# Where the unit triangular inverse and the Newton steps of the reciprocal root keep their data

## The chip, the cores and the metric

The kernel runs on one core of a Trainium2 chip. A core has five engines that run their own instruction streams in order and meet at semaphores: TensorE (PE) multiplies matrices into PSUM, VectorE (DVE) and ScalarE (ACT) do elementwise work and reach both the large memory SBUF and the small accumulator memory PSUM, GpSimd (POOL) does elementwise work in SBUF alone, and SyncE (SP) issues most DMAs. DMAs move data between DRAM and SBUF. The metric is the device time of one execution in microseconds.

## The reference

One inference step of a two-layer recurrent trunk, for 1024 prompt rows and 8 samples of 8 rows (1088 rows of width 1024). Layer 0 has an S5 state space group and a gated delta net (GDN) side by side; layer 1 is RWKV-7 time mixing. Each is followed by a gated feed-forward block (FFN) of width 2816. Two things in it matter here.

First, GDN solves, for every chunk and head, with a unit lower triangular matrix; RWKV, done in chunks of 64 rows, needs the same:

```python
tmat = lax.linalg.triangular_solve(eye + lmat, jnp.broadcast_to(eye, lmat.shape),
                                   left_side=True, lower=True)
```

Second, every norm multiplies by a reciprocal root, `lax.rsqrt(mean(x * x) + eps)`: the RMS norms of the layers, the norms of q, k and of GDN's output, and the group norm over each 64 columns after RWKV's recurrence.

## The kernel before, in words

The rows are worked on in two halves (columns 0 to 511 and 512 to 1087 of transposed activations). Dense products take float32 weights as a high and a low part and run three matmuls for each pair (`mm`, line 322). To make the parts, ScalarE rounds a weight tile `raw` to `wh` (line 305), and GpSimd subtracts, `wl = raw - wh` (line 309), until a low part has been stored in DRAM and can be loaded in later passes.

The recurrences run in units: 8 units for GDN (4 heads, 2 halves) and 32 for RWKV (8 pairs of heads, 4 segments of time, each half of the rows having two segments). The instructions of the units and of dense work are written one after the other, and a scheduler with a simulated timeline then interleaves them when the kernel is built: on each engine, rows of a unit stand between rows of the FFN or of projections. The order is fixed before the kernel runs. The 16 RWKV units of the first half run beside layer 0's second FFN half, the 16 of the second half beside layer 1's first FFN half.

Each unit calls `Kern.inverse` (line 155). It takes the 16x16 diagonal blocks `D` out of the matrix, sends them through DRAM (`dA`) so that one block lies in one partition (`L`, 32 to 40 partitions of 256 numbers), and inverts all blocks at once by substitution: `T` starts as 16x16 identities (line 181), and 15 steps of two VectorE instructions each follow, a product into a scratch tile `Tm` (line 186) and an update of `T` in place (line 188), 15 to 64 numbers a partition. That makes 30 dependent instructions for an inverse, 1200 in all. `T` goes back through DRAM (`dT`, line 190) into `Tc`, and TensorE, VectorE and ScalarE combine blocks to 32, 64 and 128 (`py`, `tt`, `TT`). `L`, `T` and `Tm` are all in SBUF. The `py` tiles of PSUM have a tag (`gi`, `gp`, `qi`) with one buffer.

`Kern.rsqrt` (line 325) finds reciprocal roots on VectorE: an estimate from the bits of the number (two integer instructions, lines 336 and 337), then three Newton steps of three instructions each (lines 340 to 342), with the estimate `y` and a scratch `q` (whose tile is also called `g`). It is called 20 times for the layers' norms (tiles `nrm...`, 64 to 72 numbers a partition, from the PSUM tile `ss`), 32 times after RWKV's units (tiles `rgn...`, 4 to 6 numbers, out of `vr`), and 18 times elsewhere (`gq`, `go`, `kn`). All its tiles but the input `ss` lie in SBUF.

Some lines serve for comparison: 519 (`al = s*0.5 - ah`, VectorE, both tensors in SBUF), 534 (`x = x + pd`, one tensor in SBUF, one in PSUM), 1657, 1692 and 1034 (VectorE reading PSUM), 1655 (ScalarE copying from PSUM).

Of the kernel before, what the change touches and what calls it, by code (L numbers as in the profile page):

```python
# [8 lines left out]
F32 = mybir.dt.float32  # L9
F32R = mybir.dt.float32r  # L10
I32 = mybir.dt.int32
AF = mybir.ActivationFunctionType
OP = mybir.AluOpType
AX = mybir.AxisListType
PSUM = bass.MemoryType.PSUM
DRAM = bass.MemoryType.DRAM

T = 1088
NP = 1024
CW = 272  # L20
NCH = [(c, CW) for c in range(0, T, CW)]

# [82 lines left out]
class Kern:  # L105
# [49 lines left out]
    def inverse(self, gp, ps, dr, A, wd, nu, ns, sgn, tag, pb=2, own=False, TT=None):  # L155
# [4 lines left out]
        nc, v = self.nc, self.nc.vector  # L160
        nl = 8 * nu + ns
        op = OP.subtract if sgn > 0 else OP.add
        dA = dr.tile([nu + 1, 8, 256], F32, name="dA", tag="dA%d" % wd)
        size = {"mk": 320, "L": 256, "T": 256, "tt32": 160, "Y32": 160}
        kin = {"Y32": "L", "tt32": "T"}
        two = [lambda n, i=i: gp.tile([128, size[kin.get(n, n)] if own else 320], F32, name=n,
                                      tag="i" + kin.get(n, n) if own else "inv%d" % i, bufs=1) for i in range(2)]
# [9 lines left out]
            nc.sync.dma_start(dA[nu, 0:ns].rearrange("b (j i) -> (b j) i", i=16), D[0:16 * ns, nu])  # L177
        L = two[0]("L")[:8 * nu + 8, :256].rearrange("p (a b) -> p a b", b=16)
        nc.sync.dma_start(L[:nl], dA.rearrange("u b (j i) -> (u b) j i", i=16)[:nl])
        T = two[1]("T")[:8 * nu + 8, :256].rearrange("p (a b) -> p a b", b=16)  # L180
        v.tensor_copy(T[:nl], self.i16[:nl])
        m = gp.tile([8 * nu + 8, 64], F32, name="Tm", tag="invm", bufs=1)
        for j in range(15):
            n = 15 - j
            mm = m[:nl, :(j + 1) * n].rearrange("p (c i) -> p c i", i=n)
            v.tensor_mul(mm, L[:nl, j:j + 1, j + 1:16].to_broadcast([nl, j + 1, n]),  # L186
                         T[:nl, 0:j + 1, j:j + 1].to_broadcast([nl, j + 1, n]))
            v.tensor_tensor(T[:nl, 0:j + 1, j + 1:16], T[:nl, 0:j + 1, j + 1:16], mm, op=op)  # L188
        dT = dr.tile([nu + 1, 8, 256], F32, name="dT", tag="dT%d" % wd)
        nc.sync.dma_start(dT.rearrange("u b x -> (u b) x")[:nl], T[:nl].rearrange("p c i -> p (c i)"))  # L190
        Tc = gp.tile([128, nu + 1, 16], F32, name="Tc", tag="invTc", bufs=1 + own)
        nc.sync.dma_start(Tc[:, 0:nu], dT[0:nu].rearrange("u b (c i) -> (b c) u i", i=16))
        TS = None
# [19 lines left out]
        py = ps.tile([128, 2, nu, 16], F32, tag=tag, name="py", bufs=pb)  # L213
# [4 lines left out]
        for u in range(nu):  # L218
            for b in range(4):
# [3 lines left out]
                               op1=OP.add)  # L223
# [16 lines left out]
        py = ps.tile([128, nu, 32], F32, tag=tag, name="py2", bufs=pb)  # L240
# [7 lines left out]
        py = ps.tile([128, 2 if wd == 128 else 1, nu, 32], F32, tag=tag, name="py3", bufs=pb)  # L248
# [15 lines left out]
        py = ps.tile([128, 2, nu, 64], F32, tag=tag, name="py4", bufs=pb)  # L264
# [57 lines left out]
                self.nc.tensor.matmul(ps, a[k], b[:, c:c + cn], start=i == 0, stop=i == last)  # L322
                i += 1

    def rsqrt(self, pool, out, x, scale, eps, tag):

        nc = self.nc
        sh = list(x.shape)
        if scale is None:
            v = x  # L330
        else:
            v = pool.tile(sh, F32, tag=tag + "v", name=tag + "v", bufs=1)
            nc.vector.tensor_scalar(v, x, scale, eps, op0=OP.mult, op1=OP.add)
        y = pool.tile(sh, F32, tag=tag + "y", name=tag + "y", bufs=1)
        g = pool.tile(sh, I32, tag=tag + "q", name=tag + "g", bufs=1)
        nc.vector.tensor_scalar(g, v.bitcast(I32), 1, None, op0=OP.logical_shift_right)
        nc.vector.tensor_scalar(y.bitcast(I32), g, -1, 0x5F3759DF, op0=OP.mult, op1=OP.add)
        q = g.bitcast(F32)
        for i in range(3):
            nc.vector.tensor_mul(q, y, y)  # L340
            nc.vector.scalar_tensor_tensor(q, q, -0.5, v, op0=OP.mult, op1=OP.mult)
            self.last = nc.vector.scalar_tensor_tensor(out if i == 2 else y, q, 1.5, y, op0=OP.add, op1=OP.mult)

    def stats(self, xs):
# [19 lines left out]
    def norm(self, ss, qn):  # L364
        p = self.dx
        r = p.tile([128, self.width // 4], F32, tag="rst", name="rst", bufs=2)[:, :qn]
        self.rsqrt(p, r, ss[:, :qn], 1.0, 1e-6, "nrm")
        return r

    def spread(self, r):  # L370
# [835 lines left out]
class RWKV:  # L1206
# [53 lines left out]
    def open(self, ctx):  # L1260
# [20 lines left out]
        nc.vector.memset(self.halo[:, 0], 0.0)  # L1281

    def projections(self, s, x, shift0, w1, a1, g1, lw2, wk, wr, wv, unit,
                    norms, wk0):

# [152 lines left out]
        for j, wt, dst, more in ((0, wr, self.drr, {1: (0,), 2: (1,), 3: (2, 3), 4: (4, 5), 5: (6, 7)}), (3, wv, self.dv, {})):  # L1438
            hs = [mix(j, i) for i in range(2)]
            if j == 3:  # L1440
                banks = banks[:2]
            for m in range(6):
                w = K.weight(wt[m])
                for i in range(2):
                    one(dst, m, w, hs[i], i)
                for ft in more.get(m, ()):
                    second(ft)
                if j == 3:
                    unit(m)
                if j == 0 and m == 0:  # L1450
                    lora(*loras[5])
                    second = self.second(s, lw2)
                if j == 0 and m == 0:
                    for i, (c, cn) in enumerate(chunks):
                        pt = self.bank("qp")[:16, :cn]
                        for y, (b, n) in enumerate(blocks[i]):
                            nc.tensor.transpose(pt[:, b:b + n], ko[:n, 3 * i + y], K.ident[:n, :n])
                        t = K.tmp("kt")[:16, :cn]
                        nc.scalar.copy(t, pt)
                        nc.sync.dma_start(dks[:, c:c + cn], t)  # L1460
            ws = [K.weight(wt[m]) for m in (6, 7)]
            for i in range(2):
                for m in (6, 7):
                    one(dst, m, ws[m - 6], hs[i], i)
        for m in (6, 7):
            unit(m)
# [79 lines left out]
    def unit(self, ft, si, s, S0):  # L1546
        K, nc, gp, HR = self.K, self.K.nc, self.gp, self.HR
        v = nc.vector
# [8 lines left out]
        def new(name, tag="up"):  # L1557
            return gp.tile([128, 320], F32, tag=tag, name=name, bufs=RING[tag])[:, :W]
# [5 lines left out]
        k, r, vv, rkb = (new(n, "ui") for n in ("k", "r", "v", "rkb"))  # L1564
# [58 lines left out]
        pb = ptile("pb")[:, :W]  # L1623
# [19 lines left out]
        for c0, n, mk in groups:  # L1643
            g = slice(c0, c0 + n)
# [25 lines left out]
        pa, pu, pb = pc[:, 0:2], pc[:, 2], pc[:, 3:5]  # L1670
        py = self.ps.tile([128, 4, 2, 64], F32, tag="qy", name="py", bufs=1)
# [6 lines left out]
        two = lambda t: t.rearrange("p a t -> p (a t)")  # L1678
# [27 lines left out]
        parts = [(slice(0, 128), slice(0, 2))] + ([(HR[0], slice(2, 3))] if smp else [])  # L1706
        yc, sq = (gp.tile([128, 3, 2, 64], F32, tag="uy", name=n, bufs=3) for n in ("yc", "sq"))
        su, vr, rs = (gp.tile([128, 3, 2], F32, tag="u_" + n, name=n, bufs=1) for n in ("su", "vr", "rs"))
        wide = lambda t, p: t[p][:, :, :, None].to_broadcast([p[0].stop, p[1].stop - p[1].start, 2, 64])
        if smp:  # L1710
            v.memset(vr, 1.0)
        for p in parts:
            v.tensor_reduce(su[p], py[p], op=OP.add, axis=AX.X)
            v.scalar_tensor_tensor(yc[p], wide(su, p), -1.0 / 64, py[p], op0=OP.mult, op1=OP.add)
            nc.scalar.activation(sq[p], yc[p], AF.Square)
            v.tensor_reduce(vr[p], sq[p], op=OP.add, axis=AX.X)
            v.tensor_scalar(vr[p], vr[p], 1.0 / 64, 64e-5, op0=OP.mult, op1=OP.add)
        nb = W // 128 + W % 128 // 64
        K.rsqrt(gp, rs[:, :nb], vr[:, :nb], None, None, "rgn")
        pT = ptile("pT", "qp", 1)[:, :W]  # L1720
        for p in parts:
            nc.gpsimd.tensor_mul(yc[p], yc[p], wide(rs, p))
# [3 lines left out]
        g = new("g", "ul")  # L1726
# [48 lines left out]
def layer0(K, I, right, dr):  # L1775
# [19 lines left out]
    with ExitStack() as c1:  # L1795
# [27 lines left out]
        with tc.tile_pool(name="x0", bufs=4, side="right") as x0, tc.tile_pool(name="psn", bufs=2, space=PSUM) as psn:  # L1823
# [15 lines left out]
            for j, (c, cn) in enumerate(NCH):  # L1839
                if j == 0:  # L1840
                    norm(c, cn)
                    wba = K.weight(I["wba"], 8, 8, tag="wba", bufs=1)
                    ws = [K.weight(I["win"][i], bufs=2) for i in range(2)]
                if j + 1 < len(NCH):
                    norm(*NCH[j + 1])
                if j == 1:
                    s5.consts(hi[7][:, c:c + 1].bitcast(F32), *(I[k] for k in ("lre", "lim", "ls", "bre", "bim", "cre", "cim", "dsk", "h0")))
                proj(wba, lambda c, cn, ps: nc.scalar.copy(rows[:, c:c + cn], ps), 8, [(c, cn)])
                for m, w in enumerate(ws):
                    inputs(m, w, [(c, cn)])  # L1850
# [266 lines left out]
```

## Time and profile before

| | |
|---|---|
| median of 3 runs | 3689.62 us (3682.62 to 3697.84) |
| the profiled execution | 3691.23 us, its span 3689.5 us |
| mean granted TensorE clock | 0.943 |
| busy: PE, DVE, ACT, POOL | 92%, 65%, 38%, 28% of the span |

Busy PE time is the union of pipelined matmuls, so 92% is not TensorE at its peak. Three stretches of the span hold all inverses: 340 to 828 us (GDN, 8 inverses), 1374 to 2116 us (RWKV, first half, 16) and 2363 to 3140 us (RWKV, second half, 16).

### The profile page before, as it was taken

To read this page: it belongs to the slowest core of one execution; us is meant where nothing else is said; L and a number is where in the kernel's file an instruction comes from. 1 tells how busy PE (TensorE), PEld (TensorE's weight loads), DVE (VectorE), ACT (ScalarE), POOL (GpSimd) and SP (SyncE) were. 2 spreads that over 40 slices of the span, in tenths; PEclk is the share of its full clock that TensorE was granted. 3 is DMA by queue.
4 is the path that set the end of the run, shared out by engine and by line. 5 is a ranking of instruction groups with operands and counts; after the bars stand their busy time and mean duration, and the time that the engine had idled before them with its cause. 6 is when DMAs were issued, how large, how long until landed. Compare 5 with 4: busy or idle time off the path is not lost.

```text
span 3689.5 us, 77380 instructions
## 1 busy us (share of the span) xinstructions
PE 3379.0 (92%) x29894; PEld 3171.2 (86%) x29894; DVE 2394.0 (65%) x6834; ACT 1390.8 (38%) x3264; POOL 1041.0 (28%) x1037
## 2 busy tenths in 40 slices
PE   7889999999997889999999898898988989899998
PEld 6879888989997888899889888888887877799997
DVE  7886888754448556776666673577778888344344
ACT  3333333323224454444443454443443444222222
POOL 3222133223216450111010142334333332122221
PEclk8989987999998899999999999989999999899998
DMA  3434453445554585344443456722322324322322
GB/s 102 95 87 120 96 177 104 130 132 188 186 174 132 176 292 161 111 143 150 153 130 114 135 167 221 238 86 87 87 82 84 102 79 135 105 69 75 92 81 66
DMA packets 387552, 474.36 MB, mean 129 GB/s; under 512 B 142312, under 2 KB 305896, under 8 KB 387184
## 3 DMA queue, kind: packets, MB, share of 16 engines
q1 hardware_dynamic: 364144, 447.13, 39.8%
q10 hardware_dynamic: 23040, 22.29, 1.8%
q8 instruction: 235, 3.85, 0.4%
q14 instruction: 133, 1.09, 0.1%
HBM read 344.32 MB, written 123.79 MB: 127 GB/s over the span
## 4 chain that ended last, share of the span: by engine, by line
PE 54%; DVE 26%; DMA 12%; issue 3%; ACT 3%; SPq 1%; POOL 1%; DVEq 0%; ACTq 0%; POOLq 0%
PE pg L322 20%; PE pd L322 10%; PE pj L322 5%; PE po L322 4%; PE pi L322 3%; DVE T L188 3%; DVE Tm L186 3%; DVE mx L1350 1%; DMA raw<-in_wd 1%; DMA dT<-T 1%; DMA L<-dA 1%; DMA rkb<-dks 1%; DMA Tc<-dT 1%; DVE x L534 1%; DVE Z L800 1%
## 5 line engine op out<-in xcount | busy, mean ns | idle before, releaser
L322 PE MATMUL pg<-hi,wh 128*128 128x288 f32 (+1 forms) x2816 | 833.8, 296 | 23.8 <-DVE s L511 15.5
L322 PE MATMUL pg<-lo,wh 128*128 128x288 f32 (+1 forms) x2816 | 830.9, 295 | 4.4 <-DVE lo L409 3.5
L322 PE MATMUL pg<-hi,wl 128*128 128x288 f32 (+1 forms) x2816 | 827.8, 294 | 1.2 <-POOL wl L309 1.2
L309 POOL TENSOR_TENSOR wl<-raw,wh 128x1024 fp32r<-128x1024 f32 (+3 forms) x205 | 483.1, 2358 | 903.5 <-ACT wh L305 791.5
L322 PEld LDWEIGHTS pg<-hi,wh 128*128 128x128 f32 x2816 | 540.7, 192 | 32.9 <-DVE s L511 19.1
L322 PEld LDWEIGHTS pg<-lo,wh 128*128 128x128 f32 x2816 | 540.8, 192 | 12.4 <-DVE lo L409 5.2
L322 PEld LDWEIGHTS pg<-hi,wl 128*128 128x128 f32 x2816 | 540.2, 192 | 3.3 <-POOL wl L309 1.4
L305 ACT CAST wh<-raw 128x1024 fp32r<-128x1024 f32 (+3 forms) x309 | 313.2, 1014 | 362.7 <-PE pg L322 99.6
L322 PE MATMUL pd<-ah,wdh 128*128 128x256 f32 (+1 forms) x1280 | 387.2, 303 | 20.3 <-DVE x L534 16.5
L322 PE MATMUL pd<-ah,wdl 128*128 128x256 f32 (+1 forms) x1280 | 373.5, 292 | 5.9 <-DMA wdl<-low_wd 5.9
L322 PE MATMUL pd<-al,wdh 128*128 128x256 f32 (+1 forms) x1280 | 371.9, 291 | 0.0
L322 PEld LDWEIGHTS pd<-ah,wdh 128*128 128x128 f32 x1280 | 243.8, 190 | 32.0 <-DVE x L534 18.2
L322 PE MATMUL pj<-hi,wh 128*128 128x256 f32 (+1 forms) x768 | 235.5, 310 | 18.1 <-ACT hi L408 7.7
L322 PEld LDWEIGHTS pd<-ah,wdl 128*128 128x128 f32 x1280 | 243.8, 190 | 9.1 <-DMA wdl<-low_wd 7.6
L322 PEld LDWEIGHTS pd<-al,wdh 128*128 128x128 f32 x1280 | 244.2, 191 | 0.4
L322 PE MATMUL pj<-hi,wl 128*128 128x256 f32 (+1 forms) x768 | 232.2, 307 | 12.7 <-DMA wl<-low_wr 7.5
L322 PE MATMUL pj<-lo,wh 128*128 128x256 f32 (+1 forms) x768 | 235.2, 308 | 8.7 <-DVE lo L409 6.8
L534 DVE TENSOR_TENSOR x<-x,pd 128x256 f32<-128x256 f32 (+1 forms) x384 | 162.4, 426 | 92.0 <-PE pd L322 88.5
L305 ACT CAST wdh<-raw 128x384 fp32r<-128x384 f32 (+1 forms) x224 | 111.2, 497 | 258.6 <-PE pd L322 161.2
L322 PE MATMUL pi<-hi,wh 128*128 128x272 f32 x640 | 191.5, 299 | 5.0 <-ACT us L1818 3.5
L186 DVE TENSOR_TENSOR Tm<-L,T 32x15 f32<-32x15 f32 (+8 forms) x600 | 161.1, 268 | 47.6 <-DMA L<-dA 34.6
L322 PE MATMUL pi<-lo,wh 128*128 128x272 f32 x640 | 190.2, 297 | 0.0
(643 smaller groups left out, 8008.2 us busy)
## 6 DMA issues: line engine op xcount, KB each, us to landing
raw<-in_wg SPq DMA_DIRECT2D x88, 512.0 KB
raw<-in_wup SPq DMA_DIRECT2D x88, 512.0 KB
raw<-in_wd SPq DMA_DIRECT2D x192, 192.0 KB
low_wg<-wl SPq DMA_DIRECT2D x22, 512.0 KB
low_wup<-wl SPq DMA_DIRECT2D x22, 512.0 KB
wl<-low_wg SPq DMA_DIRECT2D x22, 512.0 KB
wl<-low_wup SPq DMA_DIRECT2D x22, 512.0 KB
raw<-in_win SPq DMA_DIRECT2D x20, 512.0 KB
```

The source lines that it names most:

```text
L186: v.tensor_mul(mm, L[:nl, j:j + 1, j + 1:16].to_broadcast([nl, j + 1, n]), T[:nl, 0:j + 1, j:j + 1].to_broadcast([nl, j + 1, n]))
L188: v.tensor_tensor(T[:nl, 0:j + 1, j + 1:16], T[:nl, 0:j + 1, j + 1:16], mm, op=op)
L305: nc.scalar.copy(wh, raw)
L309: (lo or nc.gpsimd).tensor_sub(wl, raw, wh)
L322: self.nc.tensor.matmul(ps, a[k], b[:, c:c + cn], start=i == 0, stop=i == last)
L534: v.tensor_add(x[m][:, c:c + cn], x[m][:, c:c + cn], ps)
L800: v.tensor_add(o, o, m1)
L1350: v.scalar_tensor_tensor(t, xx[k][:, c:c + cn], self.vec[:, j, k:k + 1], x[k][:, c:c + cn], op0=OP.mult, op1=OP.add)
```

## The change

`T` of the substitution moves to PSUM, into the tag that the `py` tiles of the same inverse use. Its start, a copy of the identities, moves from VectorE to ScalarE; after the 15 steps ScalarE copies `T` to an SBUF tile `Ts`, and the DMA to `dT` reads that. `rsqrt` takes an optional `y`, and the Newton step is written so that each instruction has `y` and at most one other tensor as inputs (`q = v*y`, `q = q*-0.5*y`, `y = (q+1.5)*y`) instead of `q = y*y`, `q = q*-0.5*v`; the first shift now writes into the bits of `y`. The layers' norms give as `y` a free part of the PSUM tile `ss`, RWKV's group norm a free part of its PSUM tile `py`, which also takes the sums `vp`. The other calls keep `y` in SBUF. The number of VectorE instructions in a root stays 11.

```diff
--- before.py
+++ after.py
@@ -177,8 +177,8 @@
             nc.sync.dma_start(dA[nu, 0:ns].rearrange("b (j i) -> (b j) i", i=16), D[0:16 * ns, nu])
         L = two[0]("L")[:8 * nu + 8, :256].rearrange("p (a b) -> p a b", b=16)
         nc.sync.dma_start(L[:nl], dA.rearrange("u b (j i) -> (u b) j i", i=16)[:nl])
-        T = two[1]("T")[:8 * nu + 8, :256].rearrange("p (a b) -> p a b", b=16)
-        v.tensor_copy(T[:nl], self.i16[:nl])
+        T = ps.tile([128, 512], F32, tag=tag, name="T", bufs=pb)[:8 * nu + 8, :256].rearrange("p (a b) -> p a b", b=16)
+        nc.scalar.copy(T[:nl], self.i16[:nl])
         m = gp.tile([8 * nu + 8, 64], F32, name="Tm", tag="invm", bufs=1)
         for j in range(15):
             n = 15 - j
@@ -187,7 +187,9 @@
                          T[:nl, 0:j + 1, j:j + 1].to_broadcast([nl, j + 1, n]))
             v.tensor_tensor(T[:nl, 0:j + 1, j + 1:16], T[:nl, 0:j + 1, j + 1:16], mm, op=op)
         dT = dr.tile([nu + 1, 8, 256], F32, name="dT", tag="dT%d" % wd)
-        nc.sync.dma_start(dT.rearrange("u b x -> (u b) x")[:nl], T[:nl].rearrange("p c i -> p (c i)"))
+        Ts = two[1]("T")[:8 * nu + 8, :256]
+        nc.scalar.copy(Ts[:nl], T[:nl].rearrange("p c i -> p (c i)"))
+        nc.sync.dma_start(dT.rearrange("u b x -> (u b) x")[:nl], Ts[:nl])
         Tc = gp.tile([128, nu + 1, 16], F32, name="Tc", tag="invTc", bufs=1 + own)
         nc.sync.dma_start(Tc[:, 0:nu], dT[0:nu].rearrange("u b (c i) -> (b c) u i", i=16))
         TS = None
@@ -322,7 +324,8 @@
                 self.nc.tensor.matmul(ps, a[k], b[:, c:c + cn], start=i == 0, stop=i == last)
                 i += 1
 
-    def rsqrt(self, pool, out, x, scale, eps, tag):
+    def rsqrt(self, pool, out, x, scale, eps, tag, y=None):
+
 
         nc = self.nc
         sh = list(x.shape)
@@ -331,14 +334,15 @@
         else:
             v = pool.tile(sh, F32, tag=tag + "v", name=tag + "v", bufs=1)
             nc.vector.tensor_scalar(v, x, scale, eps, op0=OP.mult, op1=OP.add)
-        y = pool.tile(sh, F32, tag=tag + "y", name=tag + "y", bufs=1)
-        g = pool.tile(sh, I32, tag=tag + "q", name=tag + "g", bufs=1)
+        if y is None:
+            y = pool.tile(sh, F32, tag=tag + "y", name=tag + "y", bufs=1)
+        q = pool.tile(sh, F32, tag=tag + "q", name=tag + "q", bufs=1)
+        g = y.bitcast(I32)
         nc.vector.tensor_scalar(g, v.bitcast(I32), 1, None, op0=OP.logical_shift_right)
-        nc.vector.tensor_scalar(y.bitcast(I32), g, -1, 0x5F3759DF, op0=OP.mult, op1=OP.add)
-        q = g.bitcast(F32)
+        nc.vector.tensor_scalar(g, g, -1, 0x5F3759DF, op0=OP.mult, op1=OP.add)
         for i in range(3):
-            nc.vector.tensor_mul(q, y, y)
-            nc.vector.scalar_tensor_tensor(q, q, -0.5, v, op0=OP.mult, op1=OP.mult)
+            nc.vector.tensor_mul(q, v, y)
+            nc.vector.scalar_tensor_tensor(q, q, -0.5, y, op0=OP.mult, op1=OP.mult)
             self.last = nc.vector.scalar_tensor_tensor(out if i == 2 else y, q, 1.5, y, op0=OP.add, op1=OP.mult)
 
     def stats(self, xs):
@@ -364,7 +368,7 @@
     def norm(self, ss, qn):
         p = self.dx
         r = p.tile([128, self.width // 4], F32, tag="rst", name="rst", bufs=2)[:, :qn]
-        self.rsqrt(p, r, ss[:, :qn], 1.0, 1e-6, "nrm")
+        self.rsqrt(p, r, ss[:, :qn], 1.0, 1e-6, "nrm", ss[:, 128:128 + qn])
         return r
 
     def spread(self, r):
@@ -1706,6 +1710,7 @@
         parts = [(slice(0, 128), slice(0, 2))] + ([(HR[0], slice(2, 3))] if smp else [])
         yc, sq = (gp.tile([128, 3, 2, 64], F32, tag="uy", name=n, bufs=3) for n in ("yc", "sq"))
         su, vr, rs = (gp.tile([128, 3, 2], F32, tag="u_" + n, name=n, bufs=1) for n in ("su", "vr", "rs"))
+        vp, yp = [py[:, 3, 0, 8 * i:8 * i + 6].rearrange("p (a b) -> p a b", b=2) for i in range(2)]
         wide = lambda t, p: t[p][:, :, :, None].to_broadcast([p[0].stop, p[1].stop - p[1].start, 2, 64])
         if smp:
             v.memset(vr, 1.0)
@@ -1713,10 +1718,10 @@
             v.tensor_reduce(su[p], py[p], op=OP.add, axis=AX.X)
             v.scalar_tensor_tensor(yc[p], wide(su, p), -1.0 / 64, py[p], op0=OP.mult, op1=OP.add)
             nc.scalar.activation(sq[p], yc[p], AF.Square)
-            v.tensor_reduce(vr[p], sq[p], op=OP.add, axis=AX.X)
-            v.tensor_scalar(vr[p], vr[p], 1.0 / 64, 64e-5, op0=OP.mult, op1=OP.add)
+            v.tensor_reduce(vp[p], sq[p], op=OP.add, axis=AX.X)
+            v.tensor_scalar(vr[p], vp[p], 1.0 / 64, 64e-5, op0=OP.mult, op1=OP.add)
         nb = W // 128 + W % 128 // 64
-        K.rsqrt(gp, rs[:, :nb], vr[:, :nb], None, None, "rgn")
+        K.rsqrt(gp, rs[:, :nb], vr[:, :nb], None, None, "rgn", yp[:, :nb])
         pT = ptile("pT", "qp", 1)[:, :W]
         for p in parts:
             nc.gpsimd.tensor_mul(yc[p], yc[p], wide(rs, p))
```

The scheduler also lays out the whole program anew. On VectorE, ahead of the first inverse with 40 partitions (the ninth RWKV unit of the second half), the copy that starts `T` stands before the change among rows of this unit, of the unit before it and of the FFN (`rgn...` is the root of the unit before, `MB`, `AR`, `BG` are the unit's products, `XV` the recurrence, `x<-x,pd` the FFN):

```order
L1659 TENSOR_TENSOR BG<-pg,mk 128x4x64
L336 TENSOR_SCALAR rgng<-vr 128x4
L181 COPY T<-ii 40x256
L534 TENSOR_TENSOR x<-x,pd 128x256
L337 TENSOR_SCALAR rgny<-rgng 128x4
L1657 TENSOR_TENSOR MB<-pg,mks 64x64
```

The copy was one of VectorE's own rows, with no wait for another engine between it and the first step.

After the change it stands, for the same inverse, on ScalarE between the rows of the unit and a rounding of a weight (`wh<-raw`):

```order
L307 CAST wh<-raw 128x1024
L1687 ACTIVATE SP<-H,Pe 128x64
L1644 COPY XV<-pt 128x128
L181 COPY T<-ii 40x256
L1720 ACTIVATE sq<-yc 128x256
L1689 COPY X<-pc 64x64
```

The start of `T` is now well ahead of the substitution, in ScalarE's queue.

The new copy out of PSUM of the same inverse stands on ScalarE behind an FFN row that waits for TensorE (`s<-pg`), and before the recurrence (`XV<-pc`):

```order
L522 ACTIVATE ah<-s 128x256
L1689 COPY X<-pc 64x64
L307 CAST wh<-raw 128x1024
L514 ACTIVATE s<-pg 128x256
L191 COPY T<-T 40x256
L1692 COPY XV<-pc 64x64
L307 CAST wh<-raw 128x1024
L522 ACTIVATE ah<-s 128x256
```

The DMA to `dT`, which followed VectorE's last step directly, now follows this copy.

On VectorE the substitution still stands between rows of other work; these are its steps 6 and 7 before the change, in the same inverse (`al<-s,ah`, `s<-s,pg` are the FFN, `X<-pc` the recurrence):

```order
L186 TENSOR_TENSOR Tm<-L,T 40x60
L517 TENSOR_TENSOR s<-s,pg 128x256
L1688 COPY XV<-pc 64x64
L188 TENSOR_TENSOR T<-T,Tm 40x6x10
L186 TENSOR_TENSOR Tm<-L,T 40x63
L519 SCALAR_TENSOR_TENSOR al<-s,ah 128x256
L188 TENSOR_TENSOR T<-T,Tm 40x7x9
```

Over all 40 inverses 713 other VectorE instructions stand between first and last steps before, and 725 after.

## Rows read from the trace of the kernel before

**Rows 1.** Page: span, then busy us of each engine (share of the span), instructions.
```profile
span 3689.5 us, 77380 instructions
PE 3379.0 (92%) x29894; PEld 3171.2 (86%) x29894; DVE 2394.0 (65%) x6834; ACT 1390.8 (38%) x3264; POOL 1041.0 (28%) x1037
```

**Rows 2.** Stretches: length, busy us (instructions) of PE, PEld, DVE, ACT, POOL, clock, DMA.
```profile
340.00:828.00 488.00, 458.89 (x4063) 424.51 (x4062) 367.18 (x1118) 166.09 (x354) 130.86 (x123) 0.91 0.43 127
1374.00:2116.00 742.00, 700.63 (x6884) 662.06 (x6883) 498.40 (x1807) 326.13 (x851) 87.09 (x155) 0.98 0.45 139
2363.00:3140.00 777.00, 701.46 (x7233) 637.86 (x7236) 613.36 (x1881) 318.32 (x857) 285.27 (x270) 0.95 0.32 95
```

**Rows 3.** Same stretches, instructions on tile Tm alone (lines 186 and 188).
```profile
340.00:828.00 488.00, 61.91 (x240) 0.91 0.43 127
1374.00:2116.00 742.00, 95.60 (x480) 0.98 0.45 139
2363.00:3140.00 777.00, 161.27 (x480) 0.95 0.32 95
```

**Rows 4.** Timeline: start us, duration us, engine, line, operation, out<-in, shape.
```profile
2847.84 2.38 POOL L309 TENSOR_TENSOR wl<-raw,wh 128x1024 fp32r<-128x1024 f32 x1 [2.63 <-ACT wh L305]
2847.92 2.38 DVE L186 TENSOR_TENSOR Tm<-L,T 40x63 f32<-40x63 f32 x1
2850.34 0.22 DVE L188 TENSOR_TENSOR T<-T,Tm 40x63 f32<-40x63 f32 x1
```

**Rows 5.** By line, all executions: duration ns min/median/max, first and last start, forms.
```profile
L519 DVE SCALAR_TENSOR_TENSOR al<-s,ah x176: 371/448/2459, 646.4 to 3635.8; 128x256 fp32r<-128x256 f32 x88, 128x288 fp32r<-128x288 f32 x88
L534 DVE TENSOR_TENSOR x<-x,pd x384: 381/421/456, 719.9 to 3124.8; 128x256 f32<-128x256 f32 x128, 128x288 f32<-128x288 f32 x64
```

**Rows 6.** Chain that ended last, shares by line, in the stretches of rows 2.
```profile
by line: PE pg L322 13.7%; PE pi L322 8.6%; PE po L322 8.1%; PE pd L322 6.1%; PE pb L983 4.4%; PE pk L1112 3.4%; DVE T L188 3.1%; DVE Tm L186 2.5%; PE pk L1119 2.4%; PE pq L972 2.4%; PE pk L1151 2.3%; PE pn L1174 2.1%; issue 2.1%; PE g L108
by line: PE pg L322 17.8%; PE pd L322 12.0%; PE po L322 5.1%; DMA dT<-T 3.4%; DMA L<-dA 3.3%; DMA raw<-in_wd 3.3%; DMA Tc<-dT 2.8%; issue 2.7%; DVE Tm L186 2.7%; DVE T L188 2.6%; DMA rkb<-dks 2.5%; PE pg L1649 2.2%; DMA dA<-D 2.0%; DMA wdl<
by line: PE pg L322 13.3%; DVE Tm L186 7.8%; DVE T L188 7.5%; PE po L322 4.3%; PE pd L322 3.9%; issue 3.4%; DVE x L534 2.9%; DMA rkb<-dks 2.2%; DVE BK L1616 2.1%; DMA Tc<-dT 2.1%; DVE rgng L340 1.8%; DVE al L519 1.8%; DMA dT<-T 1.6%; DVE AR
```

**Rows 7.** Stretches, VectorE instructions on tile rgng alone (root after the units).
```profile
1374.00:2116.00 742.00, 34.27 (x176) 0.98 0.45 139
2363.00:3140.00 777.00, 46.42 (x165) 0.95 0.32 95
```

**Rows 8.** Stretches, VectorE instructions on tile nrmg alone (root of the norms).
```profile
1374.00:2116.00 742.00, 10.35 (x44) 0.98 0.45 139
3140.00:3690.00 550.00, 16.67 (x44) 0.95 0.26 81
```

**Rows 9.** By line as rows 5: substitution, and VectorE reading PSUM (L1657, L1692, L1034).
```profile
L186 DVE TENSOR_TENSOR Tm<-L,T x600: 136/198/2434, 343.0 to 3124.3; 32x15 f32<-32x15 f32 x14, 32x55 f32<-32x55 f32 x14, 32x63 f32<-32x63 f32 x14, 32x39 f32<-32x39 f32 x14
L1657 DVE TENSOR_TENSOR MB<-pg,mks x16: 206/222/229, 2735.1 to 3087.6; 64x64 f32<-64x64 f32 x16
L1692 DVE SCALAR_TENSOR_TENSOR XV<-pc,Pe,SP x192: 234/284/294, 1410.4 to 3161.7; 64x64 f32<-64x64 f32 x192
L1034 DVE TENSOR_SCALAR nq<-pq x16: 142/146/164, 311.8 to 704.5; 128x4 f32<-128x4 f32 x16
L1717 DVE TENSOR_SCALAR vr<-vr x40: 135/160/876, 1447.7 to 3169.5; 128x4 f32<-128x4 f32 x32, 64x2 f32<-64x2 f32 x8
```

**Rows 10.** By line: the copy that starts T; a ScalarE copy from PSUM.
```profile
L181 DVE COPY T<-ii x40: 271/282/1842, 340.8 to 3082.0; 32x256 f32<-32x256 f32 x28, 40x256 f32<-40x256 f32 x8, 36x256 f32<-36x256 f32 x4
L1655 ACT COPY MB<-pg x64: 347/367/369, 1359.6 to 3084.3; 64x256 f32<-64x256 f32 x64
```

**Rows 11.** Timeline of VectorE: an inverse's last step, and its return through DRAM.
```profile
2857.95 0.18 DVE L188 TENSOR_TENSOR T<-T,Tm 40x15 f32<-40x15 f32 x1
...
2862.52 0.33 DVE L203 TENSOR_TENSOR tt<-Tc,half 128x160 f32<-128x160 f32 x1 [2.23 <-DMA Tc<-dT]
```

**Rows 12.** A ScalarE wait in 2363:3128: us in total, times, longest us.
```profile
ACT s L510 <- PE pg L322: 14.1, 12, 4.1
```

## The prediction

> **What bounds the kernel now.** I read the page first, then the chain of waits by stretch, then the busy time of single tiles by stretch, and last the timeline. The page says TensorE, but loosely: 92% is the union of pipelined matmuls [rows 1]. The three stretches that hold the inverses differ [rows 2]. In the second RWKV half GpSimd is busy 285 of 777 us, in the first half 87 of 742, and VectorE 613 against 498, with the same 16 units and about as many VectorE instructions (1881 against 1807). The reader is to see that more VectorE time stands beside more GpSimd time.
>
> The substitution shows it plainest. Its 480 instructions take 95.60 us in the first half, 199 ns each, and 161.27 us in the second, 336 ns each; in GDN 61.91 us for 240, 258 ns each [rows 3]. Shapes are nearly the same, and the median of line 186 is 198 ns [rows 9], so about 199 ns is what one costs undisturbed, and the rest is a few long ones, up to 2434 ns. The timeline shows such a one [rows 4]: GpSimd's subtraction runs from 2847.84 to 2850.22 us, and a product of 63 numbers that began at 2847.92 ends at 2850.30. The next step takes 0.22 us. VectorE is held for as long as GpSimd's instruction lasts.
>
> Which instructions are held? Line 519 has both tensors in SBUF: median 448 ns, longest 2459. Line 534 in the same FFN has one in PSUM: 384 executions, median 421, longest 456 [rows 5]. So a VectorE instruction with two tensors in SBUF is held, and one with a tensor in PSUM was never held in 384 cases. Lines 186 and 188 now get their tensor in PSUM, and so do most instructions of the norms' and the group norm's roots.
>
> **What the change removes.** Against 199 ns: second half 161.27 - 480 x 0.199 = 65.7 us, GDN 61.91 - 240 x 0.199 = 14.1 us, first half nothing. How much of it is on the path? The chain gives the two lines 7.8% + 7.5% = 15.3% of 777 us, 119 us of their 161.27, or 74%; in GDN 5.6% of 488 us, 27.3 of 61.91, or 44%; in the first half 5.3% of 742 us, 39.3 of 95.60, or 41% [rows 3, 6]. That makes 65.7 x 0.74 = 48.6 and 14.1 x 0.44 = 6.2 us.
>
> The group norm's roots cost 34.27 / 176 = 195 ns an instruction in the first half and 46.42 / 165 = 281 ns in the second [rows 7]: 14.3 us, at 74% (the share of the inverse beside them) 10.6 us. The roots of the norms cost 10.35 us for 44 instructions in a middle stretch and 16.67 us for 44 in the last [rows 8]: 6.3 us, which I count whole, because the next matmuls need them. The sum is 48.6 + 6.2 + 10.6 + 6.3 = 71.7 us.
>
> Not all of this is won. GpSimd's instruction still runs, and the next VectorE row with two SBUF tensors meets it instead. Such rows (`al<-s,ah`) stand between the steps of the substitution, as the order shows, and behind it. Both ends are nothing moved and all moved; 18 rows stand between the steps of an average inverse (713 / 40) and most have a PSUM tensor, so I take one fifth: 14.3 us, which leaves 57.4 us.
>
> VectorE also loses 40 copies of 282 ns [rows 10], 11.3 us, mostly done while the DMA of `L` was under way; 3 us of it on the path.
>
> **What it adds.** The copy of `T` out of PSUM stands between the last step and the DMA. Its nearest row is the copy of 64x256 from PSUM, 367 ns [rows 10]. To this comes the wait in ScalarE's queue. It is at least nothing, and at most what the FFN row in front of it waits for TensorE, 4.1 us as the longest [rows 12]; ScalarE is busy 318 of 777 us with 857 instructions [rows 2], 0.37 us each, so it is free more often than not, and I take 0.23 us, 0.6 us in all. What it delays is the way through `dT` and `Tc`. From the last step to its return it took 2862.52 - 2858.13 = 4.4 us [rows 11], 70 us for 16. On the chain it stands with 3.4% + 2.8% of 742 = 46 us in the first half, 65% of 70, and with 1.6% + 2.1% of 777 = 29 us in the second, 41% [rows 6]; in GDN, where it isn't among the first shares, I take 25%. 16 x 0.6 x 0.65 + 16 x 0.6 x 0.41 + 8 x 0.6 x 0.25 = 11.4 us.
>
> The copy that starts `T` is covered by the DMAs of `dA` and `L`. If that cover is gone (the one `qi` bank is free only after the last product of the inverse before), it costs 0.4 us for each inverse that follows closely. The norms' `ss` bank is held some 2 us longer, for eleven instructions, while TensorE waits for this root in any case. 2 us for both together, between 0 and 16 (0.4 x 40).
>
> What VectorE pays for PSUM itself is not shown, least of all for writing there, which no row does. Reading: 222 ns for 64 numbers with one tensor in PSUM (line 1657), against 198 as the median of steps of 15 to 64 numbers in SBUF; a small `tensor_scalar` 146 ns from PSUM (line 1034) against 160 ns in SBUF (line 1717); with a scalar operand too 284 ns (line 1692), 62 more than without [rows 9]. Hence bounds of -14 and +62 ns an instruction. I take 0, as the nearest rows lie on both sides of it. On the path are 240 x 0.44 + 480 x 0.41 + 480 x 0.74 = 658 steps, 176 x 0.41 + 176 x 0.74 = 202 instructions of the group norm and 220 of the norms, 1080 together: -15 to +67 us.
>
> **Sum.** 57.4 + 3 - 11.4 - 2 = 47.0 us. The profiled execution took 3691.2 us, 1.6 us above the median of the runs. 3691.2 - 47.0 = 3644.2, and on the median's footing, which every time below has too, 3642.6 us. What is late next in the second half: the recurrence and the DMA round trips, which are the chain of the first half already.
>
> **Rivals.** *A, the stall was cover:* the chain is one path of several, TensorE is called busy 701 of 777 us [rows 2], and other waits take over; only a quarter of 71.7 us is won: 17.9 + 3 - 11.4 - 2 = 7.5 us, 3682 us. Against it: the second half needs 35 us more than the first though it has the smaller FFN half beside it, and the held steps alone explain more than that.
>
> *B, PSUM costs VectorE its upper bound* in read-modify-write steps, 62 ns: 67 - 47.0 = 20 us lost, 3710 us. For it: line 1692's 284 ns; against it: lines 1657 and 1034. [...]
>
> *C, slower, through ScalarE's queue:* the copy of `T` stands behind rows that wait for TensorE, and its DMA becomes the path. At 4.1 + 0.37 = 4.47 us for each of the 32 RWKV copies, on the path for 65% in the first half and now 74% in the second as the steps ahead of it are: 46.5 + 52.9 = 99 us instead of 10, so 89 us more, 3732 us. It decides from a copy of (47.0 + 10.2) / (16 x 0.65 + 16 x 0.74) = 2.6 us, a wait of 2.2 us in the queue. For it: the order shown puts `s<-pg` right ahead; against it: that wait came 12 times in the stretch, 14.1 us in all [rows 12].
>
> **How the numbers follow.** Forecast 0.70, A 0.14, B 0.06, C 0.10. The forecast's own range, from nothing moved, copies at 0.4 us and PSUM at -14 ns to two fifths moved and copies at 1.5 us, runs from 71.7 + 3 - 7.6 + 15 = 82 us won, 3607 us, to 43.0 + 3 - 28.5 - 2 = 15.5 us won, 3674 us; if the stalls were wholly on the path (65.7 x 0.26 + 14.1 x 0.56 + 14.3 x 0.26 = 29 us), still lower. For 8 in 10 I go from 3595 to 3688, which leaves out B, C and the lowest end. A measurement can tell about 0.5% from no change, 3671 to 3708. Faster: the forecast's 0.69 and a third of A, 0.74; same: the rest of A, a third of B and a little of C, 0.14; slower: 0.12.
>
> **What would show it.** Right: lines 186 and 188 near 200 ns in all three stretches, with no long ones, some 96 us in the second half in place of 161; the roots near 195 ns; a shorter third stretch, the first RWKV stretch hardly changed; line 519's mean a little higher. The new copy some 0.37 us, its DMA on the chain in the first half a little more. Wrong: long ones remaining in lines 186 and 188 (a tensor in PSUM is not enough), a median of 260 ns (B), ScalarE's copy waiting microseconds (C), or short steps and an unchanged stretch (A).

## The result, and the profile after

The changed kernel takes 3650.51 us (median of 4 runs, 3644.14 to 3658.13) against 3691.42 us (4 runs) for the one before, run beside it, a ratio of 0.9894 with a 95% interval of [0.9873, 0.9914], as in brackets behind every ratio below: faster by 41 us, where 47 were forecast and 3642.6 us named. The profiled execution took 3658.13 us, the longest of the four.

The page's busy times of the changed kernel, with their share of the span and the count of instructions:

```profile
PE 3372.0 (92%) x29894; PEld 3166.5 (87%) x29894; DVE 2287.9 (63%) x6794; ACT 1420.2 (39%) x3344; POOL 1036.2 (28%) x1037
```

TensorE and GpSimd are within 0.5% of before [rows 1]. VectorE is busy 106 us less, of which the 40 removed copies explain 11; ScalarE makes them now, and the copy back.

The substitution alone, on tile `Tm` by stretch (us from the start, length, busy time, count, granted clock, DMA share, GB/s); the stretches hold the same inverses as in [rows 3]:

```profile
340.00:830.00 490.00, 46.51 (x240) 0.91 0.43 125
1394.00:2136.00 742.00, 92.47 (x480) 0.98 0.46 139
2369.00:3115.00 746.00, 93.25 (x480) 0.96 0.34 102
```

The 161.27 us of the second RWKV half have become 93.25, 193 to 194 ns an instruction in all three stretches. From the first step of that half to the last it takes 726 us (2369.8 to 3095.6), where it took 761 (2363.6 to 3124.8). The rows of both lines, over all executions, answer to [rows 9] (duration min/median/max):

```profile
L186 DVE TENSOR_TENSOR Tm<-L,T x600: 148/193/215, 342.6 to 3094.7; 32x15 f32<-32x15 f32 x14, 32x55 f32<-32x55 f32 x14, 32x63 f32<-32x63 f32 x14, 32x39 f32<-32x39 f32 x14
L188 DVE TENSOR_TENSOR T<-T,Tm x600: 158/203/225, 342.8 to 3095.4; 32x15 f32<-32x15 f32 x14, 32x55 f32<-32x55 f32 x14, 32x63 f32<-32x63 f32 x14, 32x39 f32<-32x39 f32 x14
```

The maxima tell the story: 2434 ns before, 215 and 225 ns now. A piece of the timeline shows the same meeting as [rows 4], without the hold (start us, duration us, engine, line):

```profile
2377.90 2.39 POOL L311 TENSOR_TENSOR wl<-raw,wh 128x1024 fp32r<-128x1024 f32 x1 [0.20 <-ACT wh L307]
2378.06 0.20 DVE L186 TENSOR_TENSOR Tm<-L,T 32x60 f32<-32x60 f32 x1
2378.30 0.22 DVE L188 TENSOR_TENSOR T<-T,Tm 32x60 f32<-32x60 f32 x1
```

Nine instructions of the substitution begin and end beside this one subtraction of GpSimd. The roots lost their long instructions too: the group norm's scratch tile by stretch, which answers to [rows 7],

```profile
1394.00:2136.00 742.00, 22.15 (x144) 0.98 0.46 139
2369.00:3150.00 781.00, 22.41 (x144) 0.95 0.33 100
```

and the layers' norms' scratch, which answers to [rows 8]:

```profile
1394.00:2136.00 742.00, 8.14 (x36) 0.98 0.46 139
3122.00:3657.00 535.00, 8.22 (x36) 0.96 0.26 81
```

Nine instructions of a root touch this tile, eleven did before. The two stretches now cost the same: 154 and 156 ns an instruction for the group norm, where it was 195 and 281, and 226 and 228 ns for the norms, where it was 235 and 379. In the chain of waits of the second half (2369 to 3115 us) the two lines, 15.3% before [rows 6], are no longer among the first shares (0.8% each):

```profile
by line: PE pg L324 19.8%; PE pd L324 12.0%; PE po L324 5.8%; issue 4.1%; PE pg L1653 3.0%; DMA Tc<-dT 2.6%; DMA dT<-T 2.4%; DVE al L523 2.2%; DMA rkb<-dks 2.1%; DVE BK L1620 1.9%; PE pc L1685 1.5%; DVE tt L205 1.4%; PE pn L1774 1.3%; PE pc
```

What moved up are the FFN's products and the way through DRAM. Two rows of VectorE with only SBUF tensors stand there too: `DVE al`, 1.8% before, has 2.2%, and `DVE tt` was not among the first shares before. They now meet GpSimd's subtraction more often: `al` takes over 700 ns in 46 of its 176 executions, 33 before, and `tt` in 9 of 40, 4 before. One inverse of that half shows it, together with ScalarE's new copy (timeline):

```profile
2987.86 0.17 DVE L188 TENSOR_TENSOR T<-T,Tm 40x15 f32<-40x15 f32 x1
2988.11 0.35 ACT L191 COPY T<-T 40x256 f32<-40x256 f32 x1
...
2992.05 2.40 POOL L311 TENSOR_TENSOR wl<-raw,wh 128x1024 fp32r<-128x1024 f32 x1 [1.24 <-ACT wh L307]
2992.13 2.50 DVE L205 TENSOR_TENSOR tt<-Tc,half 128x160 f32<-128x160 f32 x1
```

The copy starts 0.07 us after the last step and takes 0.35 us; then `tt`, 0.33 us in [rows 11], lasts 2.50 us and ends 0.18 us after GpSimd.

### The profile page after: what moved, and what is told of

Its sections match the earlier page's. It is cut to its first block, busy times and chain, and to the rows that moved or that the text cites. A ratio compares the mean times of both kernels' runs of the same rounds, so it can differ in the third digit from the quotient of the medians.

```text
span 3656.4 us, 77453 instructions
## 1 busy us (share of the span) xinstructions
PE 3372.0 (92%) x29894; PEld 3166.5 (87%) x29894; DVE 2287.9 (63%) x6794; ACT 1420.2 (39%) x3344; POOL 1036.2 (28%) x1037
## 5 line engine op out<-in xcount | busy, mean ns | idle before, releaser
L324 PE MATMUL pj<-hi,wh 128*128 128x256 f32 (+1 forms) x768 | 236.7, 312 | 19.4 <-ACT st L1409 9.1
L523 DVE SCALAR_TENSOR_TENSOR al<-s,ah 128x288 fp32r<-128x288 f32 (+1 forms) x176 | 151.0, 858 | 70.8 <-ACT ah L522 70.2
L324 PE MATMUL pi<-hi,wl 128*128 128x272 f32 x640 | 191.8, 300 | 0.0
```

The costliest lines, as they stand in the source:

```text
L523: v.scalar_tensor_tensor(al[:, c:c + cn], t, 0.5, ah[:, c:c + cn], op0=OP.mult, op1=OP.subtract)
```

## The experiments

The kernels ran in three groups of four, each group on one chip beside runs of the kernel before, against which its ratios stand. The theory at first: the held substitution was the price, and its end is the gain. The first four kernels take the change apart.

**The inverse alone** (all roots back in SBUF, in their new form):

```diff
-        self.rsqrt(p, r, ss[:, :qn], 1.0, 1e-6, "nrm", ss[:, 128:128 + qn])
+        self.rsqrt(p, r, ss[:, :qn], 1.0, 1e-6, "nrm")
...
-        K.rsqrt(gp, rs[:, :nb], vr[:, :nb], None, None, "rgn", yp[:, :nb])
+        K.rsqrt(gp, rs[:, :nb], vr[:, :nb], None, None, "rgn")
```

> The change with the roots back in SBUF (y, vp in SBUF); only the inverse's T is in PSUM. Theory (a VectorE instruction with two SBUF tensors is held while GpSimd runs, one with a tensor in PSUM is not): lines 186 and 188 stay at 160 to 225 ns with no long ones, as in the changed kernel, and most of its 41 us remains: 25 to 35 us below the kernel before, 3656 to 3666 us. Rival (the gain is that of the roots, or of a program laid out anew, and the steps were cover): 0 to 10 us below, 3681 to 3691 us, though the steps are short.

Measured: 3642.77 us, 0.9878 [0.9858, 0.9898]. The inverse alone gives the whole of what the change gives, more than the 25 to 35 us expected.

**The roots alone** (`T` back in SBUF, with its copies as before; `y` of norms and group norm in PSUM):

> The change with T of the inverse back in SBUF (and its two ScalarE copies gone); only the roots of the norms and of the group norm have y in PSUM. Theory: those root instructions lose their long ones, lines 186 and 188 keep theirs (some 160 us in the second RWKV half, a little more, since GpSimd meets them instead): 8 to 15 us below the kernel before, 3676 to 3683 us. Rival (the roots carry the gain): 25 to 40 us below.

Measured: 3665.06 us, 0.9949 [0.9931, 0.9968]. Alone the roots win 0.5%, 19 us, which lies between the two ranges; beside the inverse they win nothing. The two parts don't add up.

**The copies alone** (`T` in an SBUF tile of its own, started and copied by ScalarE):

```diff
-        v.tensor_copy(T[:nl], self.i16[:nl])
+        nc.scalar.copy(T[:nl], self.i16[:nl])
...
+        nc.scalar.copy(Ts[:nl], T[:nl].rearrange("p c i -> p (c i)"))
```

> The kernel before with the two ScalarE copies of the change (the start of T, and T to Ts before the DMA) but T in SBUF: what the copies cost without what they buy. Theory: the way from the last step to tt gets 0.7 us (the forecast) to 1.5 us longer (what the changed kernel shows in the second half), so 11 to 25 us above the kernel before, 3702 to 3716 us; lines 186 and 188 keep their long ones. Rival (the longer way is covered by other work of the unit): within 5 us of the kernel before.

Measured: 3703.82 us, 1.0048 [1.0031, 1.0065], as the theory had it: in this layout the way through ScalarE costs 11 to 24 us when nothing is gained for it. What the order of the program does by itself (below) is of the same size and not in that interval.

**Only the scratch `Tm` in PSUM**: the product then writes PSUM but has two SBUF inputs, the update has one.

```diff
-        m = gp.tile([8 * nu + 8, 64], F32, name="Tm", tag="invm", bufs=1)
+        m = ps.tile([128, 512], F32, tag=tag, name="Tm", bufs=pb)[:8 * nu + 8, :64]
```

> The kernel before with only the scratch tile Tm in PSUM: line 186 reads two tensors from SBUF and writes PSUM, line 188 reads T from SBUF and Tm from PSUM and writes SBUF; no copies are added. Theory (two SBUF inputs are what is held): line 186 keeps long ones up to 2.4 us, line 188 has none over 0.3 us; some 130 us in place of 161 in the second half, 5 to 20 us below the kernel before. Rival (the hold is on the writing side, or any PSUM operand frees an instruction): line 186 has no long ones; under the writing side line 188 keeps its long ones.

Measured: 3672.31 us, 0.9961 [0.9945, 0.9977], 12 us less, within the range. Its rows by line, and one meeting on its timeline:

```profile
L186 DVE TENSOR_TENSOR Tm<-L,T x600: 149/209/2427, 339.3 to 3108.8; 32x15 f32<-32x15 f32 x14, 32x55 f32<-32x55 f32 x14, 32x63 f32<-32x63 f32 x14, 32x39 f32<-32x39 f32 x14
...
L188 DVE TENSOR_TENSOR T<-T,Tm x600: 147/192/214, 339.5 to 3109.4; 32x15 f32<-32x15 f32 x14, 32x55 f32<-32x55 f32 x14, 32x63 f32<-32x63 f32 x14, 32x39 f32<-32x39 f32 x14
```

```profile
2560.87 2.40 POOL L309 TENSOR_TENSOR wl<-raw,wh 128x1024 fp32r<-128x1024 f32 x1 [0.63 <-ACT wh L305]
2560.92 2.43 DVE L186 TENSOR_TENSOR Tm<-L,T 32x60 f32<-32x60 f32 x1
```

The product is held though it writes PSUM; the update, which reads one tensor there, never is (214 ns at most). So the product with two SBUF inputs is held also where its output lies in PSUM (2427 ns at most).

The next four ask what a better version would look like.

**The change without the layers' norms in PSUM** (only the first of the two hunks of the inverse alone), to see what it costs that the bank `ss` is held through the root:

> The whole change but for the layers' norms, whose y goes back to SBUF (the group norm's stays in PSUM). The inverse alone came out at 0.9878 of the kernel before, the whole change at 0.9894, though the roots alone win 0.5%. Theory 1 (the norms hold the ss bank until the root is done, and dense work waits for the bank): without that the time falls under both, 0.984 to 0.987. Theory 2 (stalls freed in the group norm's root are not on the path any more once the inverse is short): 0.987 to 0.990, like the inverse alone.

Measured: 3611.44 us, 0.9809 [0.9788, 0.9829], the fastest of all, 31 us below the changed kernel by ratio and below both ranges. It looked like a proof that the bank's hold costs 31 us; the last four kernels try that.

**`L` and `Tm` in PSUM, `T` in SBUF**, from the fifth step on, so that no copy is on the way back:

```diff
+        nc.scalar.copy(Lp[:nl], L[:nl])
...
+            m, Lj = (m0, L) if j < 4 else (pm[:, 256:320], Lp)
```

> The kernel before with T in SBUF as it was, but from the fifth step on L (copied to PSUM by ScalarE while the first four steps run) and Tm in PSUM; the first four steps run in SBUF. No copy of T, neither at the start nor at the end. Theory (two SBUF inputs are held, and the copy of T costs on the way back): 22 of 30 instructions of an inverse have no long ones, lines 186 and 188 keep about a quarter of their stall, the way from the last step to tt is that of the kernel before (4.4 us in the second half, not 5.7), and the time is 0.983 to 0.988 of before, at or below the inverse alone. Rival (the fifth step waits for ScalarE's copy of L as long as the copy of T cost): the spans of the inverses lengthen, 0.989 to 0.994.

Measured: 3665.12 us, 0.9954 [0.9936, 0.9972], which misses both ranges. The first four steps keep their holds (33 of them over 400 ns, in lines that had 81 before), and the fifth step starts 0.40 us after the fourth on average, 0.22 us before, so a part of the hop stands there now, some 7 us in 40 inverses. Why the rest isn't won is not shown: from its first step to its last the second half takes 722 us here, as little as the changed kernel's 726.

**The copy back on VectorE** in place of ScalarE, on top of the inverse alone:

```diff
-        nc.scalar.copy(Ts[:nl], T[:nl].rearrange("p c i -> p (c i)"))
+        v.tensor_copy(Ts[:nl], T[:nl].rearrange("p c i -> p (c i)"))
```

> The inverse alone in PSUM, with the copy of T to SBUF at the end on VectorE instead of ScalarE. Theory (ScalarE's queue is part of the price: the copy began 0.37 us late on the mean, up to 1.6 us): the way from the last step to tt falls from 5.7 to 5.2 us in the second half, and the time is 0.2 to 0.5% below that of the inverse alone, 0.983 to 0.986 of before. Rival (VectorE's 40 copies of 0.4 us cost what the queue cost): as the inverse alone, 0.986 to 0.990.

Measured: 3662.21 us, 0.9943 [0.9923, 0.9963], above both ranges and slower than with ScalarE's copy. From the last step to `tt` it takes 5.95 us on average in the second half, against 5.69: the way back did not get shorter. What cost the rest is not shown.

**The FFN's product in its PSUM bank**, on top of the inverse alone, so that `al`, the row that takes most of the moved holds, has one SBUF input too (`ah` and `al` then read `ps` in place of `t`):

```diff
-            v.tensor_mul(t, t, ps)
+            v.tensor_mul(ps, t, ps)
...
```

> The inverse alone in PSUM, and the FFN's product s*pg written back to its PSUM bank, so that al = s*0.5 - ah has one tensor in PSUM too. Theory (the stall that left the inverse went to al<-s,ah, mean 810 ns against a median of 457, 62 us in all): its long ones go, and 10 to 35 us of them are won on top of the inverse alone, 0.978 to 0.985 of before. Rival (TensorE waits for its two banks, which are held through ScalarE's and VectorE's next instruction): 0.99 or more, with TensorE waiting for al.

Measured: 3675.56 us, 0.9973 [0.9956, 0.999], in the rival's range. The hold went, and the time is longer than with the inverse alone all the same. `al` with the inverse alone, then in this kernel:

```profile
L523 DVE SCALAR_TENSOR_TENSOR al<-s,ah x176: 372/457/2429, 645.4 to 3591.2; 128x256 fp32r<-128x256 f32 x88, 128x288 fp32r<-128x288 f32 x88
L523 DVE SCALAR_TENSOR_TENSOR al<-pg,ah x176: 401/431/459, 643.1 to 3621.8; 128x256 fp32r<-128x256 f32 x88, 128x288 fp32r<-128x288 f32 x88
```

And two waits of TensorE for `al` (total us, times, longest), which it does not have with the inverse alone:

```profile
PE pg L324 <- DVE al L523: 13.3, 6, 4.7
PE pd L324 <- DVE al L523: 5.8, 12, 1.5
```

`al` is never over 459 ns, 75 us of VectorE's held time are gone against the inverse alone, and yet 33 us are lost: `pg` is free only after `al`, and TensorE waits 13.3 us for it, and 5.8 us for `al` as an input. Fourteen of the 33 us these rows don't explain; the order may (below).

The last four test the 31 us of the norms. Theory 1: the held bank costs them. Rival 2: the operand in PSUM does. Rival 3: neither, the scheduler lays the whole program out anew for each version, and the difference falls as it may.

**The bank held, `y` in SBUF** (one more VectorE row behind each norm's root):

```diff
+        self.nc.vector.tensor_copy(p.tile([128, 1], F32, tag="nrmh", name="nrmh", bufs=1), ss[:, 0:1])
```

> The version without the layers' norms in PSUM, and behind each of their 20 roots one more VectorE copy of a single column of the bank `ss`: the running estimate stays in SBUF, but the bank is held to the end of the root as in the changed kernel (20 instructions of at most 0.2 us, 4 us at most). Theory 1 (holding the bank costs the 31 us between the changed kernel and the version without): 3638 to 3655 us, ratio to before 0.987 to 0.992. Rival 2 (the operand in PSUM costs it, not the hold): 3610 to 3620, 0.980 to 0.983. Rival 3 (neither: the order that the scheduler lays out differs, and the difference falls as it may): anywhere from 0.979 to 0.992, with the roots themselves no longer than before.

Measured: 3634.38 us, 0.9879 [0.9859, 0.9898]. That speaks against rival 2; between theory 1 and rival 3 it doesn't decide.

**Only the norms in PSUM**, everything else as before:

> Before, with nothing changed but the running estimate of the layers' norms in the bank `ss`. Theory 1 (holding the bank costs 31 us): slower than before by about that, ratio 1.005 to 1.010. Rival 2 (the operand in PSUM costs it): the same, 1.005 to 1.010. Rival 3 (the order): the roots gain their held time, up to 6 us, and the order adds what it may: 0.994 to 1.004.

Measured: 3683.69 us, 1.0007 [0.9993, 1.0022]: no change. Theory 1 and rival 2 wanted 1.005 at least.

**A neutral edit on the changed kernel, and the same on the version without the norms**:

```diff
-            if k % 2:
+            if not k % 2:
                 nc.vector.tensor_mul(sq[:, :cn], x, x)
```

> The changed kernel, with a neutral edit: of the eight squares that each norm takes, ScalarE makes those that VectorE made and the other way round (four of eight each, as before), so work and banks are the same and only the order is laid out anew. Theory 1 and rival 2: 0.988 to 0.991, as the changed kernel (0.9894). Rival 3: off its twin by 0.3% or more on either side.

> The same neutral edit on the version without the layers' norms in PSUM (0.9809). Theory 1 and rival 2: 0.980 to 0.983, so 0.006 to 0.010 under its partner with the norms in PSUM. Rival 3: off its twin by 0.3% or more, and the distance to the partner with the norms in PSUM is no longer 0.0085: under 0.004, or of the other sign.

Measured: 3629.63 us, 0.9867 [0.9848, 0.9886], and 3625.58 us, 0.9855 [0.9833, 0.9876]. With the same work laid out in another order, the changed kernel is 0.27% faster, a little less than rival 3 wanted and with an interval that overlaps its twin's; the other is 0.46% slower, its interval clear of its twin's, and the distance between the two falls from 0.0085 to 0.0012. Rival 3 stands, on one twin of each: most of the 31 us was the order. The stretch from the end of the second half's first inverse to that of its last shows it, one row for each kernel (busy time with counts of PE, PEld, DVE, ACT, POOL; granted clock). The changed kernel, and its twin with the neutral edit:

```profile
2402.00:3122.00 720.00, 673.66 (x7129) 614.39 (x7128) 528.10 (x1824) 318.42 (x864) 270.44 (x258) 0.95 0.33 99
```

```profile
2376.00:3088.00 712.00, 663.93 (x7146) 606.35 (x7143) 525.32 (x1825) 318.51 (x864) 272.26 (x258) 0.97 0.33 100
```

The version without the norms, and its twin:

```profile
2366.00:3062.00 696.00, 656.61 (x7094) 598.74 (x7093) 521.68 (x1804) 316.95 (x860) 273.53 (x258) 0.97 0.33 99
```

```profile
2369.00:3090.00 721.00, 668.99 (x7141) 609.64 (x7136) 530.70 (x1825) 318.57 (x864) 272.84 (x258) 0.96 0.33 99
```

The last two differ by 25 us with nearly the same counts, and by a neutral edit alone.

## Why the prediction was right

**The hold and its remedy: right.** None of the 1200 instructions of the substitution is long in any of the eight kernels with `T` in PSUM (225 ns at most), though in the changed kernel 205 of them begin and end inside one GpSimd instruction, and the second half's `Tm` time is 93.25 us for the 96 named. The word "a tensor in PSUM" was loose: with its output alone there, in the kernel with only `Tm` in PSUM, the product still took up to 2427 ns; the tensor has to be an input.

**The price of PSUM, taken as 0: right.** The product, which reads `T` there, has a median of 193 ns for 198 [rows 9], the update, which reads and writes there, 203 ns for 199, by its row of before:

```profile
L188 DVE TENSOR_TENSOR T<-T,Tm x600: 140/199/2421, 343.2 to 3124.6; 32x15 f32<-32x15 f32 x14, 32x55 f32<-32x55 f32 x14, 32x63 f32<-32x63 f32 x14, 32x39 f32<-32x39 f32 x14
```

Rival B's 62 ns are not in these rows.

**Where the holds go, "one fifth": perhaps too little.** Count for each VectorE instruction what it takes above the lower quartile of its line and shape. In the two lines of the substitution this fell from 89.9 to 3.1 us, in the roots from 63.4 to 22.2, with the starting copies 2.9 more: 131 us. Everything else rose from 273.0 to 313.6, so 31% came back, `al` (59.2 to 73.8) and the split's `lo` (19.4 to 31.8) ahead, and `tt`, which stands on the way back itself (3.8 to 11.4). On the prediction's 71.7 us that is 22 in place of 14.3. But the kernel before is the lowest of its kind: counted the same way, everything else is 286 to 297 us in the five other kernels with `T` in SBUF and 304 to 320 in the seven with `T` in PSUM and the FFN as it was. Mean against mean that is some 24 us, about a fifth of what was freed. So 31% is the upper reading, and the fifth is not refuted.

**ScalarE's copy, 0.6 us and 11.4 in all: too little in this trace.** Its row:

```profile
L191 ACT COPY T<-T x40: 345/362/369, 352.4 to 3095.8; 32x256 f32<-32x256 f32 x28, 40x256 f32<-40x256 f32 x8, 36x256 f32<-36x256 f32 x4
```

The copy was sized rightly. The wait ahead of it is 0.37 us on average (0.03 to 1.6), not 0.23. From the last step to `tt` it takes 5.99 us on average in the first half (5.39 before), 5.86 in the second (4.36) and 6.10 in GDN (5.09): longer by 0.6, 1.5 and 1.0 us. Why it is more than the copy and its wait in the second half, 0.75 us, isn't shown; with the copies alone the way there grows by 0.5 us. At the prediction's shares that is 16 x 0.6 x 0.65 + 16 x 1.5 x 0.41 + 8 x 1.0 x 0.25 = 18 us; the copies alone measured 11 to 24, in one layout. Rival C wanted 2.2 us in the queue for each copy; the longest single wait was 1.6.

**The roots of the norms, "6.3 us, which I count whole, because the next matmuls need them": not borne out.** The held time went (379 to 228 ns an instruction), and the kernel with this part alone is no faster (1.0007). The reason given holds as far as it goes: TensorE's matmuls that spread a norm's root (line 376 in the kernel before, 378 in the one with only the norms in PSUM) wait for it, in total us and times:

```profile
  PE pj L376: 9.3, 2
  PE bc L376: 7.4, 7
...
  PE bc L378: 3.4, 2
  PE pj L378: 3.3, 1
```

These waits fall by 10 us, and the time does not. Other parts of that kernel got longer, GDN's inverses for one: 463 us from the first step to the last, in place of 438. So the step from "the matmuls wait" to "the whole is won" isn't shown by any run, and 6.3 us is less than the order moves. The group norm's 10.6 us can't be told either: the inverse alone is as fast as the whole change.

**GDN's 6.2 us: not seen.** Its 240 instructions lost 15.4 us (61.91 to 46.51), but from the first to the last the stretch takes 449 us in the changed kernel and 438 before. Over the kernels it takes 429 to 449 us with `T` in PSUM and 438 to 464 with `T` in SBUF, so the order hides the term.

**The sum.** With the two sizes as this trace has them it is 71.7 - 22 + 3 - 18 - 2 = 33 us, and without the norms' roots some 27 us; the medians have 41, and the mean of the changed kernel and its twin (0.9880) 44. That the profiled executions are 33 us apart (3691.2 and 3658.1) proves nothing, as the later one is the longest of its four. So the sum explains some two thirds to four fifths of the gain, the shares of the path (74, 44 and 41%) were tested by no run alone, and that the forecast's 47 lies so close to 41 is partly luck: the order is worth as much as its errors. Rival A, a quarter won, is out: TensorE's busy time hardly moved, but the second half's inverses take 35 us less, and five times A's 7.5 us was won.

Open stays why inverse and roots don't add up (0.9878 and 0.9949 alone, 0.9894 and 0.9867 together). With a scatter of 0.3 to 0.5% from the order, a part of 17 us isn't resolved by one layout of each version. What is beyond it, as groups: the six versions with `T` in PSUM, ScalarE's copies and the FFN as it was lie from 0.9809 to 0.9894, and all with `T` in SBUF from 0.9949 to 1.0048. The second half shows the same from the first step to the last: 710 to 736 us in the eight kernels with `T` in PSUM, 739 to 772 in the five with `T` and `L` in SBUF, and 722 in the one with `L` in PSUM from the fifth step on.

## What to carry to other kernels

Look for VectorE rows whose maximum is ten times the median and that end when a GpSimd row ends: here, with 2434 ns for a median of 198, giving one of two SBUF inputs a place in PSUM took the hold away (225 ns at most) and changed the instruction itself by 7 ns less to 4 ns more. Count it only where the held row stands on the path, and see which bank must now stay full and which rows with two SBUF inputs come next. Where a scheduler lays the program out anew for each edit, time a neutral edit first: it tells how small a gain can be read at all.

## What the runs showed of the hardware

- Each of the 150 VectorE instructions of the substitution and the roots that took over 150 ns more than usual in the kernel before ended 11 to 116 ns after the end of a GpSimd instruction; in the kernel with only `Tm` in PSUM, the 22 products over 1500 ns ended 32 to 90 ns after GpSimd's subtraction.
- Writing PSUM cost a product of two SBUF tensors 11 ns (209 for 198), reading one tensor there saved 5 to 7 ns (193 for 198, 192 for 199). For 256 to 288 numbers, `al` with one input in PSUM has a median of 431 ns, for 457 with both in SBUF.
- At the shortest of the 40 hand-overs of `T` in the changed kernel, ScalarE started 33 ns after the end of the VectorE instruction that it waited for.
